# GpSimd's scalings written with a second operation, times one, in a hybrid SSD, attention and FFN layer

## The chip, the cores and the metric

The kernel runs on one core of one Trainium2 chip, as one launch. Its time is device microseconds (us). The median of three runs of the kernel before is 1222.43 us (1222.42 to 1225.11).

## What is computed

One layer of an encoder trunk over 1024 tokens of width 1024, in float32: a modulated RMSNorm, one input projection, a Mamba-2 SSD group of 8 heads beside a chunked attention group of 8 heads, an output projection, a second modulated RMSNorm, a gated feed-forward part with a short causal convolution, and a final RMSNorm. The change lies in two places of it:

```python
def rmsnorm(x, w):
    y = xf * lax.rsqrt(jnp.mean(xf * xf, axis=-1, keepdims=True) + EPS)
...
def chunk_attention(q, k, v, rel_bias):
    scores = jnp.einsum('bcqhd,bckhd->bhcqk', qc, kb) * (ATTN_HEAD_DIM ** -0.5)
    scores = jnp.where(valid, scores + bias[:, None], jnp.finfo(jnp.float32).min)
    p = jax.nn.softmax(scores, axis=-1)
    o = jnp.einsum('bhcqk,bckhd->bcqhd', p, vb)
```

A query sees its own chunk of 64 keys and the 8 chunks before it. The division of the exponentials by their sum, and the addition of EPS to a mean square, are the two operations that the change touches.

## The kernel before

Float32 matrix products are made of three (or two) products of rounded parts: each operand is split into a high and a low part, `mm3` (L75 to L78) issues the three matmuls, and `split` (L80 to L86) makes the parts, as a rule the high part on ScalarE (L85) and the low part on VectorE (L86), in a few calls on GpSimd.

The program has these stages, by the start times of the trace: norm and modulation and the first projections for q, k and v (0 to 103 us); attention over four pairs of heads (103 to 283 us), with the remaining q, k and v projections (`gemm_part`, accumulator `acc`) mixed in; the SSD's convolutions, its projection z and its scan (to about 580 us); the output projection and the feed-forward part (to the end).

Attention for a pair p runs over 8 query tiles of 128 tokens and two heads, 16 probability tiles for each pair and 64 in all. For each tile `attn_scores` does this, with n the number of keys, 128, 256, 384, 512 and then four times 640:

- TensorE: scores into PSUM (`s`, L262), in two buffers;
- VectorE: adds the bias, negates and keeps the row's extreme, from PSUM into the tile `p` in SBUF (L413);
- ScalarE: the exponential in place, and its sum by row (L416);
- VectorE: the reciprocal of that sum, 128x1 (L418);
- GpSimd: the tile times that reciprocal, in place, 128xn (L419).

`attn_pv` then transposes two query tiles of a head on TensorE (`tp`, L445 and L448), splits them on ScalarE and VectorE (`pt`, L85 and L86), multiplies them with the values (`pv`, L456 and L457) and adds two halves into `ya` (L461, L462). `p` has 8 buffers, `s`, `tp` and `tl` have 2, `acc` and `pv` have 1.

GpSimd does besides: two memsets for each of the 8 bias tiles (L475, L476), the low part of six weight tiles in the attention stage (L86, `wl`), and for the norms `rstd` (L113): EPS added to a 128x1 column (L116) and then that column to the power of -0.5 (L117). `rstd` is called for the 8 row tiles of the first norm (L300) and the 8 of the SSD's norm. The second and the final norm use `rstd2`, which adds on VectorE and isn't touched.

The order on each engine's queue isn't that of the source alone: the kernel is built with `schedule_with_timeline_sim=True`, where a planner puts the instructions of all engines in order by costs that it has for each of them, under the dependencies. An engine works its queue strictly in that order.

Of the kernel before, what the change touches and what calls it, by code (L numbers as in the profile page):

```python
# [13 lines left out]
ALU = mybir.AluOpType  # L14
# [50 lines left out]
def tile_block(ctx: ExitStack, tc: tile.TileContext, x, crep, pk, w_ada, w_first, w_ft, w_z,  # L65
# [3 lines left out]
    G = nc.gpsimd  # L69
# [36 lines left out]
    def stat(n=1):  # L106
        if stc[0] + n > 64:
            stc[0] = 0
        a = st1[:, stc[0]:stc[0] + n]
        stc[0] += n  # L110
        return a

    def rstd(ms, eps=EPS):  # L113
        n = ms.shape[-1]
        r = stat(n)
        G.tensor_scalar(ms, ms, eps, None, op0=ALU.add)  # L116
        G.tensor_tensor(r, ms, mhalf[:, 0:n], ALU.pow)  # L117
        return r

# [132 lines left out]
    def scores(p, i):  # L252
        d = qk[p]
        j0 = max(0, i - 4)
        n = (i - j0 + 1) * P
        off = (j0 - (i - 4)) * P
        parts = [(0, n)] if n <= 512 else [(0, 320), (320, 320)]
        st = [s_tile(), s_tile()]
        for h in range(2):
            for pi, (a, w) in enumerate(parts):  # L260
                for ti, kn in enumerate(("kh", "kl")):
                    T.matmul(st[h][:, 512 * pi:512 * pi + w], d["q"][h][:, i * P:(i + 1) * P],  # L262
                             d[kn][h][:, j0 * P + a:j0 * P + a + w], start=ti == 0, stop=ti == 1)
        return st, n, off, parts
# [31 lines left out]
    def norm1(st):  # L296
        ms = stat()
        junk = s0.tile([P, D], F32, tag="junk", name="junk")
        norm_to(xts[st], junk, ms)
        r = rstd(ms)  # L300
        V.tensor_scalar(xts[st], xts[st], r, None, op0=ALU.mult)
# [93 lines left out]
    def p_tile():  # L395
        return pp.tile([P, 640], F32, tag="p", name="p")
# [4 lines left out]
    def attn_scores(p, i, bt):  # L401
        st, n, off, parts = s00 if p + i == 0 else scores(p, i)
        res = []
        for h in range(2):
            pt_ = p_tile()
            nm, rs = stat(), stat()
            if len(parts) == 1:
                src, bsl, dst = st[h][:, 0:n], bt[h][:, off:off + n], pt_[:, 0:n]
            else:
                src = st[h].rearrange("p (a b) -> p a b", a=2)[:, :, 0:320]  # L410
                bsl = bt[h].rearrange("p (a b) -> p a b", a=2)
                dst = pt_.rearrange("p (a b) -> p a b", a=2)
            V.tensor_tensor_reduce(out=dst, in0=src, in1=bsl, scale=-1.0, scalar=3e38,  # L413
                                   op0=ALU.add, op1=ALU.min, accum_out=nm)
            pv_ = pt_[:, 0:n]
            A.activation(pv_, pv_, AF.Exp, scale=-1.0, bias=nm, accum_out=rs)  # L416
            rr = stat()
            last_v[:] = [V.reciprocal(rr, rs).ins]  # L418
            G.tensor_scalar(pv_, pv_, rr, None, op0=ALU.mult)  # L419
            res.append(pt_)  # L420
        return res

# [46 lines left out]
    def attention(p, extra=()):  # L469
        extra = dict(extra)  # L470
        bt = []
        for h in range(2):
            t = bp.tile([P, 640], F32, tag="bias", name="bias")
            nc.sync.dma_start(t, bias[2 * p + h])
            G.memset(t[0:64, 576:640], -1e30)  # L475
            G.memset(t[64:128, 0:64], -1e30)  # L476
            bt.append(t)
        for u in range(4):
            pa = attn_scores(p, 2 * u, bt)
            pb = attn_scores(p, 2 * u + 1, bt)  # L480
            for fn in extra.get(u, ()):
                fn()
            if p == 3:
                if u < 2:
                    early[4 + 2 * u] = wu_pair(w_ft[4 + 2 * u], A, G)
                for _ in range(MODS[u]):
                    mod_col(todo.pop(0), mtq[len(todo) % 4], last_v[0])
            for h in range(2):
                attn_pv(p, u, h, pa[h], pb[h])
# [345 lines left out]
    def ssd_norm(c, y, t, at=None):  # L835
        with tc.issue_after(at) if at else ExitStack():
            V.tensor_tensor(y, y, zs[:, c, 0:512], ALU.mult)
        ms = stat()
        A.activation(t, y, AF.Square, accum_out=ms)
        r = rstd(ms, 512.0 * EPS)  # L840
        A.activation(y, y, AF.Copy, scale=r)
# [708 lines left out]
```

## Time and profile before

| | |
|---|---|
| median of 3 runs | 1222.43 us |
| profiled execution: span on the core | 1221.2 us |
| instructions | 15631 |
| TensorE matmul (PE) busy | 1167.3 us, 96% |
| VectorE (DVE) busy | 928.8 us, 76% |
| ScalarE (ACT) busy | 592.0 us, 48% |
| GpSimd (POOL) busy | 174.3 us, 14% |
| L419, 64 instructions | 99.0 us |
| L116, 16 instructions | 6.4 us |

The result gives no time of the profiled execution beside its span; the span is 1.2 us below the median of the timed runs. Shares are averages over stages that differ: most of GpSimd's 174.3 us lie between 103 and 283 us. In the rows of the views, a line number stands for a line of the kernel, `out<-in` are the tiles by name, and the engine named behind an arrow is the one whose work ended the wait.

### The profile page before, as it was taken

How to read it: one execution, taken by the hardware profiler on the slowest of the kernel's cores; microseconds unless marked ns; L12 is line 12 of the kernel's file. 1: busy time of each engine (PE TensorE's matmuls, PEld its weight loads, DVE VectorE, ACT ScalarE, POOL GpSimd, SP SyncE). 2: the span in 40 equal slices, each digit the busy share in tenths (PEclk: the TensorE clock that was granted, in tenths of full speed). 3: DMA queues.
4: the chain of work that ended last, by engine and by line, in shares of the span. 5: the costliest groups of instructions: out<-in, count | busy, mean ns of one | idle time of the engine just before them, and what ended most of it. 6: DMA issues, size and time to landing. Idle time of an engine off the chain costs nothing.

```text
span 1221.2 us, 15631 instructions
## 1 busy us (share of the span) xinstructions
PE 1167.3 (96%) x5802; PEld 974.5 (80%) x5802; DVE 928.8 (76%) x1402; ACT 592.0 (48%) x993; POOL 174.3 (14%) x166
## 2 busy tenths in 40 slices
PE   5998899989999989999999999999999999999995
PEld 3877787878889978888788888888888888888884
DVE  7846454686697678657999988898889769666976
ACT  4636454664243766676544543344343445433443
POOL 1205463672000125200000000000000000000001
PEclk9999999999999999999999999999999999999998
DMA  9722211311476200141223223322233278633533
GB/s 331 259 56 63 66 54 46 111 58 51 164 246 229 88 18 35 61 147 52 70 104 118 93 107 113 129 79 86 95 129 112 108 250 305 242 126 116 171 114 137
DMA packets 56395, 150.86 MB, mean 124 GB/s; under 512 B 5632, under 2 KB 5760, under 8 KB 54912
## 3 DMA queue, kind: packets, MB, share of 16 engines
q1 hardware_dynamic: 49264, 125.49, 30.4%
q10 hardware_dynamic: 7056, 24.38, 5.0%
q8 instruction: 45, 0.74, 0.2%
q14 instruction: 30, 0.25, 0.1%
HBM read 116.56 MB, written 29.10 MB: 119 GB/s over the span
## 4 chain that ended last, share of the span: by engine, by line
PE 82%; DVE 9%; ACT 3%; issue 2%; DMA 2%; POOL 1%; SPq 0%; DVEq 0%; POOLq 0%; ACTq 0%
PE dn L76 6%; PE dn L77 6%; PE dn L78 6%; PE wops L699 5%; PE uY L76 4%; PE uY L78 4%; PE uY L77 4%; PE uX L78 3%; PE uX L76 3%; PE uZ L77 3%; PE uZ L76 3%; PE uX L77 3%; PE uZ L78 3%; PE s L76 3%; PE s L77 3%; PE s L78 3%
## 5 line engine op out<-in xcount | busy, mean ns | idle before, releaser
L77 PE MATMUL dn<-w 128*128 128x512 f32 x308 | 112.6, 391 | 0.0
L76 PE MATMUL dn<-w 128*128 128x512 f32 x308 | 112.6, 391 | 0.0
L931 POOL TENSOR_TENSOR st<-st,mhalf 128x1 f32<-128x1 f32 x16 | 10.9, 683 | 696.1 <-DVE st L930 684.6
L419 POOL TENSOR_SCALAR p<-p,st 128x640 f32<-128x640 f32 (+4 forms) x64 | 99.0, 1560 | 43.7 <-DVE st L418 36.4
L78 PE MATMUL dn<-w 128*128 128x512 f32 x308 | 103.7, 390 | 0.0
L76 PE MATMUL uY<-tH,w 128*128 128x512 f32 x248 | 97.2, 392 | 0.0
L77 PE MATMUL uY<-tL,w 128*128 128x512 f32 x248 | 97.0, 391 | 0.0
L78 PE MATMUL uY<-tH,w 128*128 128x512 f32 x248 | 96.9, 391 | 0.0
L85 ACT ACTIVATE w<-ya 128x1024 fp32r<-128x1024 f32 (+1 forms) x41 | 39.2, 956 | 87.4 <-PE uY L78 84.2
L699 PE MATMUL wops<-hH,yhl 128*128 128x512 f32 x224 | 74.1, 399 | 2.9 <-DVE yhl L86 1.5
L76 PEld LDWEIGHTS dn<-w 128*128 128x128 f32 x308 | 57.8, 188 | 12.9
L78 PEld LDWEIGHTS dn<-w 128*128 128x128 f32 x308 | 57.8, 188 | 12.8
L77 PEld LDWEIGHTS dn<-w 128*128 128x128 f32 x308 | 57.8, 188 | 12.7
L85 ACT ACTIVATE w<-xs 128x1024 fp32r<-128x1024 f32 (+1 forms) x41 | 39.1, 953 | 37.3 <-PE uY L78 33.3
L78 PEld LDWEIGHTS uY<-tH,w 128*128 128x128 f32 x248 | 46.5, 188 | 10.5
L76 PEld LDWEIGHTS uY<-tH,w 128*128 128x128 f32 x248 | 46.6, 188 | 10.3
L77 PEld LDWEIGHTS uY<-tL,w 128*128 128x128 f32 x248 | 46.6, 188 | 10.2
L413 DVE CUSTOM_DVE_ANT_0 p<-s,bias 128x640 f32<-128x640 f32 (+4 forms) x64 | 40.4, 651 | 17.5 <-PE tp L445 5.2
L76 PE MATMUL s<-hH,wh 128*128 128x512 f32 x128 | 50.1, 392 | 2.2 <-ACT xst L518 2.0
L86 DVE TENSOR_TENSOR pt<-tp,pt 128x512 fp32r<-128x512 f32 (+2 forms) x72 | 41.5, 595 | 13.1 <-ACT pt L85 12.8
L699 PEld LDWEIGHTS wops<-hH,yhl 128*128 128x128 f32 x224 | 41.8, 188 | 12.2 <-DVE yhl L86 1.9
L1101 DVE SCALAR_TENSOR_TENSOR a<-cv,pkt,a 128x1023 f32<-128x1023 f32 (+1 forms) x40 | 51.0, 1278 | 0.1
(453 smaller groups left out, 3388.9 us busy)
## 6 DMA issues: line engine op xcount, KB each, us to landing
wos<-in_w_ada_dram SPq DMA_DIRECT2D x25, 512.0 KB, 4.5
gz<-a ACTq DMA_DIRECT2D x10, 1024.0 KB, 5.0
ya<-in_w_up_dram SPq DMA_DIRECT2D x11, 768.0 KB, 4.1
xs<-in_w_up_dram SPq DMA_DIRECT2D x11, 768.0 KB, 4.2
adat<-in_w_ada_dram SPq DMA_DIRECT2D x16, 512.0 KB, 5.9
raws<-in_w_ft_dram SPq DMA_DIRECT2D x14, 512.0 KB, 4.0
gy<-a ACTq DMA_DIRECT2D x10, 512.0 KB, 2.6
qk<-in_x_dram SPq DMA_DIRECT2D x8, 512.0 KB, 6.6
```

Of the source, the lines that this page charges most:

```text
L76: T.matmul(ps, lh, rh, start=start, stop=False, skip_group_check=more)
L77: T.matmul(ps, lh, rl, start=False, stop=False, skip_group_check=more)
L78: T.matmul(ps, ll, rh, start=False, stop=stop, skip_group_check=more)
L85: i = A.activation(hi, src, AF.Copy) if ehi is A else ehi.tensor_copy(hi, src)
L86: return i, elo.tensor_tensor(lo, src, f32(hi), ALU.subtract)
L413: V.tensor_tensor_reduce(out=dst, in0=src, in1=bsl, scale=-1.0, scalar=3e38, op0=ALU.add, op1=ALU.min, accum_out=nm)
L419: G.tensor_scalar(pv_, pv_, rr, None, op0=ALU.mult)
L699: i = op(*a, **k)
L931: G.tensor_tensor(r, ms, mhalf[:, 0:1], ALU.pow)
L1101: V.scalar_tensor_tensor(a[:, j:S], c[:, 0:S - j], w[2 - j], a[:, j:S], op0=ALU.mult, op1=ALU.add)
```

## The change

Two GpSimd instructions get a second operation, a multiplication by the constant 1.0, in the same instruction. Their number, their operands in memory and what they compute stay.

```diff
@@ rstd @@
-        G.tensor_scalar(ms, ms, eps, None, op0=ALU.add)
+        G.tensor_scalar(ms, ms, eps, 1.0, op0=ALU.add, op1=ALU.mult)
         G.tensor_tensor(r, ms, mhalf[:, 0:n], ALU.pow)
...
@@ attn_scores @@
             last_v[:] = [V.reciprocal(rr, rs).ins]
-            G.tensor_scalar(pv_, pv_, rr, None, op0=ALU.mult)
+            G.tensor_scalar(pv_, pv_, rr, 1.0, op0=ALU.mult, op1=ALU.mult)
```

The planner has another order for the changed program. On TensorE it is the same up to the first attention pair and again from the SSD scan's first tiles on; between these, rows are moved on all engines, and none is added or left out.

TensorE, the first attention pair, behind the scores of its first query tiles: L262 makes scores, L445 and L448 transpose `p` for the two query tiles of a pass, L456 and L457 multiply with the values. Before:

```order
L262 MATMUL s<-qk 128x320 x2
L445 MATMUL tp<-ident,p 128x128
L262 MATMUL s<-qk 128x320 x6
L445 MATMUL tp<-ident,p 128x128
L262 MATMUL s<-qk 128x320 x4
L456 MATMUL pv<-pt,v 128x256
L457 MATMUL pv<-pt,v 128x256
L456 MATMUL pv<-pt,v 128x128
L457 MATMUL pv<-pt,v 128x128
L262 MATMUL s<-qk 128x320 x4
L448 MATMUL tp<-ident,p 128x128
L445 MATMUL tp<-ident,p 128x128
```

The same place after the change:

```order
L445 MATMUL tp<-ident,p 128x128
L262 MATMUL s<-qk 128x320 x4
L445 MATMUL tp<-ident,p 128x128
L448 MATMUL tp<-ident,p 128x128
L445 MATMUL tp<-ident,p 128x128
L448 MATMUL tp<-ident,p 128x128 x3
L262 MATMUL s<-qk 128x320 x4
L456 MATMUL pv<-pt,v 128x256
L457 MATMUL pv<-pt,v 128x256
L456 MATMUL pv<-pt,v 128x128
L457 MATMUL pv<-pt,v 128x128
L262 MATMUL s<-qk 128x320 x8
```

The transposes of the fourth query tile (L448), which stood behind two more score tiles and a product with the values, now stand directly behind the L445 of the same pass. Further on, the first transposes of the third pass (tile `p_1085` by the numbered names) now stand ahead of the second half of the `acc` product of the first `gemm_part`, where they stood behind it.

GpSimd, the end of the first pair and the start of the second, as one piece of the difference, with the buffers' numbers (`p_1195` and `p_1200` are the last tiles of the first pair, `p_1289` to `p_1310` the first of the second; `wl_1323` is the low part of a weight tile, `bias_1856` a bias tile):

```order
 L419 TENSOR_SCALAR p_1195<-p_1195,st1_72 128x640
+L476 MEMSET bias_1856 64x64
 L419 TENSOR_SCALAR p_1200<-p_1200,st1_72 128x640
-L475 MEMSET bias_1856 64x64
-L476 MEMSET bias_1856 64x64
+L419 TENSOR_SCALAR p_1289<-p_1289,st1_72 128x128
 L86 TENSOR_TENSOR wl_1323<-raws_68,wh_1605 128x1024
-L419 TENSOR_SCALAR p_1289<-p_1289,st1_72 128x128
 L419 TENSOR_SCALAR p_1294<-p_1294,st1_72 128x128
 L419 TENSOR_SCALAR p_1305<-p_1305,st1_72 128x256
 L419 TENSOR_SCALAR p_1310<-p_1310,st1_72 128x256
-L86 TENSOR_TENSOR wl_1323<-raws_68,wh_1903 128x1024
```

The memsets of a bias tile come ahead of the last scalings, the first scaling of the second pair passes the weight split, and the next weight split falls behind two more scalings.

## The prediction

> **What bounds the kernel now.** I read the page first, from its sums to the chain, to see which engine sets the end.
>
> ```profile
> PE 1167.3 (96%) x5802; PEld 974.5 (80%) x5802; DVE 928.8 (76%) x1402; ACT 592.0 (48%) x993; POOL 174.3 (14%) x166
> POOL 1205463672000125200000000000000000000001
> PE 82%; DVE 9%; ACT 3%; issue 2%; DMA 2%; POOL 1%; SPq 0%; DVEq 0%; POOLq 0%; ACTq 0%
> ```
>
> TensorE is busy for 96% of the span and makes 82% of the chain that ended last; GpSimd makes 1% of it. So the kernel is bound by TensorE, and a change on GpSimd can only be worth what TensorE now loses by waiting for it, or would lose. The row of tenths says where that can be: GpSimd works between the fourth and the tenth slice, the attention stage. The table of stages cuts that part out.
>
> ```profile
> 103.00:120.00 17.00, 13.49 (x82) 10.78 (x80) 13.45 (x47) 14.15 (x37) 15.19 (x16) 1.00 0.00 1
> 120.00:137.00 17.00, 15.40 (x85) 13.22 (x86) 7.40 (x22) 7.40 (x16) 11.79 (x11) 1.00 0.12 40
> 137.00:185.00 48.00, 45.78 (x276) 39.33 (x274) 26.60 (x73) 27.86 (x65) 26.84 (x20) 1.00 0.24 66
> 185.00:245.00 60.00, 55.88 (x320) 47.94 (x320) 32.99 (x89) 33.44 (x76) 31.38 (x22) 0.97 0.25 83
> 245.00:270.00 25.00, 21.40 (x149) 18.07 (x148) 22.04 (x65) 19.63 (x49) 18.02 (x15) 1.00 0.14 52
> 270.00:283.00 13.00, 13.00 (x68) 11.03 (x67) 9.69 (x20) 3.55 (x8) 11.80 (x5) 1.00 0.14 48
> ```
>
> Behind the window and its length stand the busy times of PE, PEld, DVE, ACT and POOL, then the granted clock. TensorE is idle for 17.00 - 13.49 = 3.51 us in the first row, then 1.60, 2.22, 4.12, 3.60 and 0: 15.05 us in all. That is the ceiling of any gain in attention, 1.2% of the time. In the first row GpSimd is the busiest engine of the core (15.19 of 17 us); in the next four it has 28% to 48% to spare, and in the last TensorE is full anyway.
>
> Next, the waits. First what TensorE's idle time is put down to in 103 to 120 us, then the three largest in 137 to 245 us, then the largest in 245 to 270 us.
>
> ```profile
> PE s L262 <- DVE st L413: 2.7, 7, 0.7
> PE tp L445 <- POOL p L419: 0.7, 1, 0.7
> ```
>
> ```profile
> PE acc L76 <- DVE qk L239: 2.2, 4, 0.8
> PE acc L76 <- DVE qk L232: 1.3, 2, 0.8
> PE s L262 <- DVE st L413: 1.0, 3, 0.4
> ```
>
> ```profile
> PE tp L448 <- DVE pt L86: 1.2, 2, 0.7
> ```
>
> TensorE names GpSimd once, for 0.7 us; the rest is VectorE, which frees score buffers, accumulators and transposes. GpSimd is behind that only in so far as late tiles put VectorE's later work off. GpSimd's own queue shows how near it is to the bound in the first pair:
>
> ```profile
> 103.84 0.63 POOL L419 TENSOR_SCALAR p<-p,st 128x128 f32<-128x128 f32 x1 [0.34 <-DVE st L418]
> 105.99 0.93 POOL L419 TENSOR_SCALAR p<-p,st 128x256 f32<-128x256 f32 x1 [0.47 <-DVE st L418]
> 107.51 17.65 POOL L419 TENSOR_SCALAR p<-p,st 128x256 f32<-128x256 f32 x11 [0.59 <-DVE st L418]
> 125.54 3.75 POOL L419 TENSOR_SCALAR p<-p,st 128x640 f32<-128x640 f32 x2
> ```
>
> From 107.51 us on eleven scalings run without a gap, two memsets, and two more until 129.29 us: GpSimd is the limit of the first pair, and TensorE escapes it because the queue has `acc` products in between.
>
> **The change, part by part: the duration.** No instruction is added, so the first question is what one GpSimd tensor_scalar costs with its second slot filled. The trace has no such instruction. The nearest rows are these:
>
> ```profile
> L419 POOL TENSOR_SCALAR p<-p,st 128x640 f32<-128x640 f32 x32 | 63.9, 2012 | 6.0 <-DVE st L418 5.1 <-PE pv L457 0.8
> L419 POOL TENSOR_SCALAR p<-p,st 128x512 f32<-128x512 f32 x8 | 13.1, 1650 | 11.1 <-DVE st L418 11.1
> L419 POOL TENSOR_SCALAR p<-p,st 128x128 f32<-128x128 f32 x8 | 4.9, 610 | 12.4 <-DVE st L418 7.2 <-PE acc L78 4.9
> L811 POOL TENSOR_TENSOR yy<-xs,pkt 128x512 f32<-128x512 f32 x8 | 10.8, 1359 | 10.1 <-PE s L77 9.9 <-PE xps L699 0.2
> L116 POOL TENSOR_SCALAR st<-st 128x1 f32<-128x1 f32 x16 | 6.4, 401 | 62.4 <-ACT junk L268 39.9 <-ACT yt L839 22.3
> masks.py:199 POOL TENSOR_SCALAR_AFFINE_SELECT ident<-ident 128x128 f32<-128x128 f32 x1 | 0.3, 294 | 0.0
> masks.py:197 POOL MEMSET ident<- 128x128 f32 x1 | 0.2, 205 | 0.3 <-POOLq L1538 0.3
> L123 POOL MEMSET mhalf<- 128x8 f32 x1 | 0.1, 105 | 0.0
> ```
>
> Two undisturbed 640s take 3.75 us, 1.87 us each; against the 610 ns of 128 columns that is (1870 - 610) / 512 = 2.46 ns for a column, over a fixed part near 0.3 us. A memset pays (205 - 105) / 120 = 0.83 ns for a column, the select, which reads, tests and writes, about (294 - 105) / 128 = 1.48 ns. And 128x512 with two inputs is shorter on average (1359 ns) than a scaling of one input (1650 ns). So the single-operation form is dear out of line with what it reads and writes: its 2.46 ns are spent in how that form is worked, and not in ports. Another form may then be worked by another loop, and the bounds lie on both sides. Below: 0.83 ns, the cheapest pass in the trace. Above: a second pass like the first, 4.92 ns. I take the select's 1.48 ns, the nearest row in kind (one input read, something computed, written). A step up of one memset pass, to 3.29 ns, is the rival below.
>
> At 1.48 ns the 64 scalings have 32 x 640 + 8 x (128 + 256 + 384 + 512) = 30,720 columns, and lose 30,720 x 0.98 ns = 30 us of GpSimd's time, 7.5 us for each pair. A 640 would take about 1.25 us.
>
> **What of that reaches the end.** First pair, 103 to 120 us: GpSimd steps down from 15.19 us by about 4,480 columns x 0.98 ns = 4.4 us to 10.8, and ScalarE is late next, with 14.15 of 17 us; that leaves 17.00 - 14.15 = 2.85 us. I take 2, since TensorE's queue also carries latencies that no engine's sum shows. 120 to 137 us: nothing, since its one long wait is for an accumulator:
>
> ```profile
> 129.57 0.47 PE L76 MATMUL acc<-hH,wh 128*128 128x512 f32 x1 [1.51 <-DVE qk L232]
> ```
>
> 137 to 245 us: 6.34 us idle, of which the two accumulator rows above are 3.5, and GpSimd doesn't touch them. The rest hangs on when VectorE comes to its splits; tiles that are ready 0.6 us earlier move that a little: I take 1. 245 to 270 us: VectorE is the busiest (22.04 of 25, so at most 2.96 us to be had), and GpSimd shortens only the way of a tile: 1. The last row: 0, TensorE is full.
>
> The sixteen additions of epsilon are 128x1, all fixed cost (L116, 401 ns on average). They stand in a chain to the norms, and a tenth of a microsecond more or less in each, by the difference between memsets of 8 and 128 columns, is at most 1.6 us either way; I take 0, since half of them are in the SSD stage, where no TensorE wait names them, and leave the 1.6 us to the range.
>
> The moved rows are the other half. The planner's new order puts transposes forward, which is only good if the tiles are there. At the old speed they nearly are: 11 scalings from 107.51 us put `p_995` at about 107.51 + 0.93 + 2 x 1.25 + 1.56 = 112.5 us, where the transposes now stand, and `p_1085` at 112.5 + 1.6 + 3 x 1.87 = 119.7 us, while the second half of the `acc` product, now behind that tile's transposes, began at 120.09 us:
>
> ```profile
> 120.09 0.50 PE L76 MATMUL acc<-hH,wh 128*128 128x512 f32 x1 [0.15 <-DVE qk L232]
> ```
>
> So the order alone costs about nothing there, 0 to 1 us, with 0.4 us of slack. Between 283 us and the SSD scan it also moves rows, with no row that says to which side; I take 0 and keep 3 us on both sides.
>
> Sum: 2 + 1 + 1 = 4 us. Span 1221.2 - 4 = 1217.2, and with the 1.2 us by which the median lies above the span, **1218.4 us**.
>
> **Rivals.** (1) The second operation costs a pass of its own. Price by the memset's slope, 0.83 ns a column. Place: the transposes of `p_1085`, ahead of the `acc` product. Before it stand 2 x (128 + 256 + 384 + 512) + 3 x 640 = 4,480 columns of scaling, 3.7 us more, against 0.4 us of slack: TensorE stands 3.3 us. It decides from 0.4 us / 4,480 = 0.09 ns a column on. The last pair, with 29.8 us of GpSimd work in the 38 us from 245 to 283, loses about 3 more in latency: 1222.4 + 6 = 1228.7 us. At the upper bound, 2.46 ns more, it is 10.6 us at the first place, and 18.9 us more work in the 8.2 us left of the last, so about 10.7 there: 1244 us. For it: GpSimd's time is in its loop. Against it: the loop is slower than any port needs, which a fuller form may not share.
>
> (2) The instruction takes as long as before, and only the order changes: 1222.4, or up to 4 us more, 1226.4, where transposes wait and the later rows move the wrong way. The Trainium skill has a rule for this (GPSIMD Engine Reference, section Performance versus the Vector engine, Elementwise — side-by-side cycle accounting): loop bodies of one or two operations on an element are bound by the ports, at 1.03 cycles for an element, so that a second one is free. At the 1.2 GHz that the page gives, that is an estimate of 0.86 ns a column. The trace doesn't agree with its rate, 2.46 ns against 0.86, so I trust its conclusion little; by it this rival would be the forecast.
>
> (3) The instruction is faster, and it is hidden: TensorE's named waits are for VectorE, and stay. 1220 to 1222 us. The waits above speak for it, the gapless first pair against it.
>
> (4) Faster, but the moved rows lose more than attention gains: 3 us in the convolutions and 3 more in the scan's first tiles, against 1 or 2: 1226.4 to 1227.4.
>
> **How the numbers follow.** The forecast has a chance of 0.50, over times from 1210 (two thirds of the 15.05 us idle) to 1218.7. Rival 3 has 0.14; rival 2 0.10, of it 0.06 within 0.3%; rival 1 0.21; rival 4 0.05. A measurement of this kernel can tell about 0.3%, 3.7 us, from no change, so the bounds are 1218.7 and 1226.1. Faster 0.50; same 0.14 + 0.06 = 0.20; slower 0.21 + 0.04 + 0.05 = 0.30. The range must take in rivals 2 to 4 and the lower half of rival 1: 1210 to 1232. What is left out, the upper half of rival 1 and the ends of the forecast's own spread, is under 0.2. The forecast's own range is 1210 to 1218.7.
>
> **What would show it.** Right, if a 128x640 of L419 is near 1.25 us and L419's 99.0 us near 69; if GpSimd has gaps in the first pair that end at L418; if 103 to 120 us holds more TensorE work than 13.49 us. The duration is wrong if L419 rises, and then TensorE waits for `p` by name at L445 ahead of `acc`. The way to the end is wrong if L419 falls and TensorE's idle time up to 270 us stays near 15 us. The order is to blame if the stages from 283 us on get longer than before.

## The result, and the profile after

The changed kernel's median is 1221.12 us (1218.42 to 1225.33, 22 runs), that of the kernel before beside it 1224.34 us (1221.96 to 1229.63, 22 runs). The ratio is 0.9973, with a 95% interval of 0.9966 to 0.9981: 0.0027 x 1224.34 = 3.3 us less. A second measurement (below) gave 0.9964 (0.9946 to 0.9982). The forecast was 4 us less. All runs here read some 2 us above the three of the table ahead, so the forecast's absolute 1218.4 us was missed by 2.7 us and its difference by 0.7.

The page of the changed kernel, its first line and GpSimd's row of tenths:

```profile
PE 1170.2 (96%) x5802; PEld 977.4 (80%) x5802; DVE 929.8 (76%) x1402; ACT 592.9 (49%) x993; POOL 123.7 (10%) x166
...
POOL 1202232440000135200000000000000000000001
```

GpSimd falls by 50.6 us, from 174.3 to 123.7, and its fourth to ninth slices from 5, 4, 6, 3, 6, 7 tenths to 2, 2, 3, 2, 4, 4. No other engine's sum moves by more than 3 us. The groups say where it went, first L419 as a whole, then by shape:

```profile
L419 POOL TENSOR_SCALAR p<-p,st 128x640 f32<-128x640 f32 (+4 forms) x64 | 45.9, 723 | 76.4 <-DVE st L418 66.2 <-PE tp L448 7.7 <-PE pv L456 1.5
```

```profile
L419 POOL TENSOR_SCALAR p<-p,st 128x640 f32<-128x640 f32 x32 | 28.2, 887 | 21.7 <-DVE st L418 19.4 <-PE pv L456 1.5 <-PE s L262 0.6
...
L116 POOL TENSOR_SCALAR st<-st 128x1 f32<-128x1 f32 x16 | 6.9, 431 | 61.1 <-ACT junk L268 40.0 <-ACT yt L839 20.9
L419 POOL TENSOR_SCALAR p<-p,st 128x512 f32<-128x512 f32 x8 | 6.4, 796 | 17.0 <-DVE st L418 15.4 <-PE tp L448 1.5
...
L419 POOL TENSOR_SCALAR p<-p,st 128x128 f32<-128x128 f32 x8 | 3.0, 372 | 10.5 <-DVE st L418 10.4
```

L419 takes 45.9 us where it took 99.0, and 66.2 of the 76.4 us of GpSimd's idle time ahead of it now end at L418, VectorE's reciprocal: GpSimd waits for tiles. Its queue in the first pair shows the same; in square brackets stands the idle time ahead of the row and what ended it.

```profile
107.97 1.04 POOL L419 TENSOR_SCALAR p<-p,st 128x256 f32<-128x256 f32 x2 [0.79 <-DVE st L418]
...
112.31 0.69 POOL L419 TENSOR_SCALAR p<-p,st 128x512 f32<-128x512 f32 x1 [2.43 <-DVE st L418]
...
117.49 0.81 POOL L419 TENSOR_SCALAR p<-p,st 128x640 f32<-128x640 f32 x1 [1.07 <-DVE st L418]
...
125.51 0.80 POOL L419 TENSOR_SCALAR p<-p,st 128x640 f32<-128x640 f32 x1
```

An undisturbed 640 takes 0.80 us, against 1.87. The pair's last scaling ends at 126.3 us, against 129.29. The stages, in the columns of the prediction's table, come from the second profiled run of the changed kernel (span 1219.0 us), because the first (1222.4 us) was, as shown below, one of the slower executions:

```profile
103.00:120.00 17.00, 14.17 (x89) 11.61 (x89) 15.51 (x54) 15.20 (x39) 8.48 (x15) 1.00 0.08 23
120.00:137.00 17.00, 15.86 (x81) 13.28 (x81) 6.79 (x19) 7.16 (x17) 5.99 (x10) 0.90 0.13 48
137.00:185.00 48.00, 45.78 (x272) 39.65 (x270) 26.57 (x71) 28.48 (x63) 15.20 (x20) 1.00 0.20 58
185.00:245.00 60.00, 56.42 (x328) 48.81 (x329) 33.12 (x93) 33.45 (x78) 18.33 (x22) 0.97 0.27 85
245.00:270.00 25.00, 22.03 (x146) 18.61 (x147) 22.41 (x66) 19.02 (x47) 10.36 (x14) 1.00 0.12 43
270.00:283.00 13.00, 13.00 (x70) 11.00 (x69) 9.89 (x17) 4.54 (x8) 5.23 (x5) 1.00 0.13 40
```

TensorE's idle time is now 2.83, 1.14, 2.22, 3.58, 2.97 and 0: 12.74 us in all, where it was 15.05. (Two of the rows, with clocks of 0.90 and 0.97, hold a stretch at half clock, in which busy time is longer for the same work; before only the fourth did.) What it waits for from 100 to 285 us, first before, then in this run of the changed kernel (us in all, times, longest):

```profile
PE s L262 <- DVE st L413: 4.7, 11, 1.1
...
PE tp L445 <- POOL p L419: 0.7, 1, 0.7
```

```profile
PE tp L445 <- POOL p L419: 1.8, 2, 1.0
PE s L262 <- DVE st L413: 1.3, 5, 0.4
```

The large wait that went is the one for score buffers, which VectorE's bias pass L413 frees: 4.7 to 1.3 us. The waits for GpSimd's own tiles did not fall; they rose from 0.7 to 1.8. Behind attention, before and then after:

```profile
283.00:411.00 128.00, 126.00 (x737) 110.23 (x736) 92.44 (x145) 49.76 (x84) 0.94 (x3) 1.00 0.53 177
```

```profile
283.00:411.00 128.00, 127.27 (x749) 111.52 (x748) 92.93 (x147) 51.48 (x92) 1.54 (x2) 1.00 0.52 177
```

Another 1.27 us of idle time is gone there (0.46 in the first profiled run, with 126.46 us busy). At the first matmul into the tile `uX`, behind the scan, the kernel before stands at 569.4 us and this run at 567.1:

```profile
L58 PE MATMUL uX<-b11h,w x16: 392/394/394, 569.4 to 574.7; 128*128 128x512 f32 x16
```

```profile
L58 PE MATMUL uX<-b11h,w x16: 393/394/394, 567.1 to 572.5; 128*128 128x512 f32 x16
```

These 2.3 us are the whole difference of the spans (1221.2 - 1219.0 = 2.2). From there to the end both take 651.8 to 651.9 us.

Fixed windows mix the gain with the moment at which a stretch begins, and with its stretches at half clock. A measure by work is cleaner: the time from TensorE's 481st matmul, just ahead of the first one that moved (the 489th), to its last product with the values (L457, at 320.4 us before), with time at half clock counted half. It is 214.2 us before, 211.0 in this run of the changed kernel and 210.7 in the first: 3.2 to 3.5 us less. From there to the first matmul into `uX` it is 247.2 us before, 247.2 in this run and 246.2 in the first. So by work the gain lies in attention, and the idle time that is gone between 283 and 411 us is no sure gain of its own. The 2.2 us between the spans are then made of 0.7 us by which this run happens to reach the 481st matmul sooner (103.8 us against 104.5; the first run is there at 105.1), plus 3.2, less 1.7 for one half-clock window more.

**Why two executions of one program differ by 3.4 us.** These are windows of 4 us on TensorE (window, length, busy time, matmuls, granted clock), first of the changed kernel's first profiled run, then of its second:

```profile
107.00:111.00 4.00, 3.69 (x14) 0.58 0.00 0
```

```profile
107.00:111.00 4.00, 4.00 (x29) 1.00 0.01 2
...
119.00:123.00 4.00, 3.25 (x9) 0.66 0.42 141
```

From 107 to 111 us the one has 14 matmuls at a mean clock of 0.58, the other 29 at 1.00, and has its own low stretch at 119 us. The 534th matmul, a transpose of the second pass, starts so, in the same order of runs (1.2 of the 2.55 us are the later start of attention; the rest goes with the low window):

```profile
116.12 0.31 PE L445 MATMUL tp<-ident,p 128*128 128x128 f32 x1
```

```profile
113.57 0.31 PE L445 MATMUL tp<-ident,p 128*128 128x128 f32 x1
```

The record of the clock has it as windows of 3.41 us, sometimes two in a row, in which the clock is 0.5. One costs up to 3.41 / 2 = 1.7 us. Before the last 15 us of the program the kernel before has two such windows in its profile, the second run of the changed kernel three, and the first run four stretches, one of them double. What comes ahead of such a window are gaps, of which none needs to be long. These are the 3.41 us just ahead of one, in the changed kernel's first run, then in the kernel before, and with it a stretch of the kernel before that no low window follows:

```profile
104.25:107.66 3.41, 1.92 (x9) 1.00 0.00 0
```

```profile
237.98:241.40 3.42, 2.29 (x15) 1.00 0.93 329
...
115.41:118.83 3.42, 2.37 (x16) 1.00 0.00 0
```

TensorE is idle for 1.49 and 1.13 us in the first two, in pieces, and for 1.05 us in the third. But the length of the idle time does not decide it alone: in the kernel before TensorE is idle for 1.71 of the 3.41 us from 333.6 to 337.0 us, in one piece, and the clock stays at 1.00 behind it. Among the timed runs of the kernel before in the second measurement, span and mean granted clock go together (correlation -0.93 over 20 runs). So below, beside each ratio, the mean of span times granted clock of the timed runs is given where it matters ("the span net of the clock"): a microsecond at half clock counts half in it, and since the clock is on record to 0.001, one run's figure is good to some 0.6 us. It is 1212.84 us before and 1209.06 us for the changed kernel in the same comparison.

### The profile page after: what moved, and what is told of

Read it like the earlier page. It is cut to its first block, busy times and chain, and to the rows that moved or that the text cites. A ratio compares the mean times of both kernels' runs of the same rounds, so it can differ in the third digit from the quotient of the medians.

```text
span 1222.4 us, 15637 instructions
## 1 busy us (share of the span) xinstructions
PE 1170.2 (96%) x5802; PEld 977.4 (80%) x5802; DVE 929.8 (76%) x1402; ACT 592.9 (49%) x993; POOL 123.7 (10%) x166
## 4 chain that ended last, share of the span: by engine, by line
PE 71%; DVE 5%; ACT 1%; DMA 1%; issue 0%; POOL 0%; DVEq 0%; POOLq 0%; ACTq 0%; SPq 0%
PE wops L699 6%; PE dn L76 6%; PE dn L77 6%; PE dn L78 6%; PE uY L76 4%; PE uY L78 4%; PE uY L77 4%; PE uX L78 3%; PE uX L76 3%; PE uZ L77 3%; PE uZ L76 3%; PE uX L77 3%; PE uZ L78 3%; PE s L76 3%; PE s L77 3%; PE s L78 3%
## 5 line engine op out<-in xcount | busy, mean ns | idle before, releaser
L413 DVE CUSTOM_DVE_ANT_0 p<-s,bias 128x640 f32<-128x640 f32 (+4 forms) x64 | 40.7, 652 | 25.3 <-PE tp L445 9.0
L419 POOL TENSOR_SCALAR p<-p,st 128x640 f32<-128x640 f32 (+4 forms) x64 | 45.9, 723 | 76.4 <-DVE st L418 66.2
```

The costliest lines, as they stand in the source:

```text
L419: G.tensor_scalar(pv_, pv_, rr, 1.0, op0=ALU.mult, op1=ALU.mult)
```

## The experiments

**1. The instruction alone.** At the end of the kernel before, 64 GpSimd instructions are added, four of each of 16 forms, on tiles of their own:

```diff
+        for o in d:
+            pin(G.tensor_scalar(o, a, r, None, op0=ALU.mult))
+        for o in d:
+            pin(G.tensor_scalar(o, a, r, 1.0, op0=ALU.mult, op1=ALU.mult))
+        for o in d:
+            pin(G.tensor_scalar(o, a, r, 0.0, op0=ALU.mult, op1=ALU.add))
+        for o in d:
+            pin(G.tensor_scalar(o, a, r, -8.0, op0=ALU.mult, op1=ALU.max))
...
```

> The kernel before with 64 more GpSimd instructions behind its end, on tiles of their own, each form four times at the end of the queue; the output is untouched and the run is some 70 us longer. What is wanted is the time of one. Theory A1 (any second operation takes the fast loop): at 128x640, one operation 1.87 us, with a column or with a constant; all pairs (times 1.0, plus 0.0, maximum) 0.80 us. Theory A2 (only a multiplication by a constant one is fast): plus 0.0 and maximum at 1.87 us or more. Theory A3 (a column as the scalar is the slow part): one operation with a constant at 0.80 us. The copy, one input and no arithmetic, near 0.6 us; a multiplication of two tiles 1.3 to 1.5 us.

The rows, `pa` the input, `pr` a column that scales it; the lines are in the order of the list that follows:

```profile
L1515 POOL TENSOR_SCALAR pd<-pa,pr 128x640 f32<-128x640 f32 x4 | 9.7, 2420 | 0.4
L1509 POOL TENSOR_SCALAR pd<-pa,pr 128x640 f32<-128x640 f32 x4 | 7.5, 1892 | 0.0
L1521 POOL TENSOR_SCALAR pd<-pa 128x640 f32<-128x640 f32 x4 | 7.2, 1815 | 0.0
...
L1511 POOL TENSOR_SCALAR pd<-pa,pr 128x640 f32<-128x640 f32 x4 | 3.1, 799 | 0.0
L1513 POOL TENSOR_SCALAR pd<-pa,pr 128x640 f32<-128x640 f32 x4 | 3.1, 798 | 0.0
...
L1523 POOL TENSOR_SCALAR pd<-pa 128x640 f32<-128x640 f32 x4 | 2.8, 723 | 0.0
L1529 POOL COPY pd<-pa 128x640 f32<-128x640 f32 x4 | 2.7, 718 | 0.0
L1533 POOL TENSOR_SCALAR pd<-pa,pr 128x128 f32<-128x128 f32 x4 | 2.3, 601 | 0.0
L1535 POOL TENSOR_SCALAR pd<-pa,pr 128x128 f32<-128x128 f32 x4 | 1.4, 372 | 0.0
L1537 POOL TENSOR_SCALAR pd<-pa 128x1 f32<-128x1 f32 x4 | 0.8, 218 | 0.0
L1539 POOL TENSOR_SCALAR pd<-pa 128x1 f32<-128x1 f32 x4 | 0.6, 190 | 0.0
```

In this order: times a column, then the maximum with -8 (2420 ns); times a column alone (1892); plus a constant alone (1815); times a column, times 1.0 (799); times a column, plus 0.0 (798); plus a constant, times 1.0 (723); a copy (718). Then 128x128 alone and with times 1.0 (601, 372), and 128x1 with an addition, alone and with times 1.0 (218, 190). A pair of multiplications or additions runs at (799 - 372) / 512 = 0.83 ns for a column, and a 640 of it takes about as long as a copy (723 to 799 against 718 ns); the single operation and the pair with a maximum take 2.4 and 3.0 times as long. None of the three theories holds as it stands: the second operation need not be a multiplication by one, but not every second operation helps. What is read and written is the same in all three, so the difference lies in how GpSimd works the form; that it is another loop is a guess that no run shows.

**2. The new form in the old order.** The changed kernel, each engine's queue held in the order of the kernel before by dependencies that carry no wait:

```diff
+ORDER = "..."
...
+def keep_order(tc):
...
+                tc.add_manual_dep(i, prev.name, mybir.DependencyInfo(
+                    mybir.DependencyClass.NoSync, mybir.DependencyReason.DATA), reason="order")
```

> The two-operation form on both lines, with every engine's queue held in the order of the kernel before. Theory A (the shorter instruction carries the gain): L419 at 128x640 stays near 0.80 us and 1.5 to 3.5 us come off, ratio 0.9971 to 0.9988. Theory B (the moved rows carry it, and a shorter instruction in the old order only makes GpSimd idle longer): 0.9992 to 1.0005, with GpSimd's gaps grown and TensorE's idle time between 103 and 270 us still near 15 us.

In the traces the kernels held like this, here and in experiments 3 and 6, have the same sequence of operations and tiles on TensorE, VectorE, ScalarE and GpSimd as the kernel whose order they hold, and as many instructions in all (15631 and 15637). So the holding itself adds no work that could explain a difference.

Measured: 0.9982 (0.9969 to 0.9995); the span net of the clock is 1212.14 us against 1212.94. By the ratio that is within theory A, and its interval overlaps that of the changed kernel. Net of the clock it is 0.8 us, where the changed kernel has 3.8 (experiment 5). Attention itself is no shorter: by the measure by work it takes 214.3 us, against 214.2 before, so where the 0.8 us lie is not shown. TensorE waits for score buffers as before:

```profile
PE s L262 <- DVE st L413: 4.8, 11, 1.4
```

**3. The old form in the new order.** The kernel before, held in the order of the changed kernel in the same way.

> The one-operation form on both lines, with every engine's queue in the order of the changed kernel. Theory A: the transposes that were put forward wait for tiles that come at 1.87 us each; the waits of L445 and L448 for L419 grow from 0.7 us to 2 to 6 us, ratio 1.001 to 1.005. Theory B: the moved rows alone give the gain, ratio near 0.997. The prediction's working has 0 to 1 us for the order at its first place, ratio 1.000 to 1.001.

Measured: 1.0019 (1.0004 to 1.0035), net of the clock 1212.80 against 1212.94 us. Its last two stages, and TensorE's waits from 100 to 285 us:

```profile
245.00:270.00 25.00, 21.87 (x137) 18.53 (x136) 19.29 (x58) 17.60 (x43) 15.70 (x14) 0.93 0.11 40
270.00:283.00 13.00, 11.21 (x57) 9.54 (x56) 10.99 (x24) 4.69 (x13) 13.00 (x6) 0.87 0.24 81
```

```profile
PE s L262 <- DVE st L413: 2.0, 5, 0.8
PE tp L448 <- POOL p L419: 1.9, 3, 1.0
```

The order takes the waits for score buffers from 4.7 to 2.0 us with the old form too. But TensorE now waits for GpSimd's tiles in their place: 1.9 us at L448, where it had no such wait, 1.2 of them in the first pair and 0.7 in the last; with 0.7 at L445, as before, that is within theory A. In the last stage GpSimd is busy for all of 13.00 us, and TensorE idle for 1.79 of a stretch that it filled before. By the measure by work attention takes 214.1 us, against 214.2 before: what one wait gives, the others take. All waits of TensorE that the view names from 100 to 285 us sum up to 14.7 us before, 14.2 in experiment 2, 14.9 here and 12.0 in the changed kernel. Each of these two stages also has a half-clock window, at 1.7 us (0.07 x 25 and 0.13 x 13).

**4. Epsilon alone, and the scalings alone.** In the first only L116 has the second operation, and the order is that of before; in the second only L419 has it, and the order is that of the changed kernel.

```diff
-            G.tensor_scalar(pv_, pv_, rr, 1.0, op0=ALU.mult, op1=ALU.mult)
+            G.tensor_scalar(pv_, pv_, rr, None, op0=ALU.mult)
```

> Only the addition of epsilon has the second operation; the order on all engines is that of the kernel before. Theory A and theory B both: ratio 0.9992 to 1.0008, since 16 instructions of 128x1 change by a tenth of a microsecond at most. A ratio under 0.9985 would mean that the norms' chain, not attention, gives part of the gain.

Measured: 0.9990 (0.9978 to 1.0002), net of the clock 1212.68 against 1212.94 us: no difference that can be told. Attention takes 214.2 us by work, as before.

```diff
-        G.tensor_scalar(ms, ms, eps, 1.0, op0=ALU.add, op1=ALU.mult)
+        G.tensor_scalar(ms, ms, eps, None, op0=ALU.add)
```

> The scaling L419 in the two-operation form, the addition of epsilon in the old form; the order of each engine is that of the changed kernel. Theory, the scalings alone make the gain: ratio 0.9960 to 0.9985, like the changed kernel's. Rival, the additions of epsilon carry part of it: ratio between 0.9985 and 1, and the changed kernel's gain is not reached.

Measured: 0.9968 (0.9956 to 0.9981), with 211.0 us for attention by work, as in the changed kernel. The scalings are the change.

**5. The changed kernel once more,** to have a second profile of it and a second ratio.

> The changed kernel itself, beside the kernel before and the variants below on one chip, to part the clock from the work: for each run, span times mean granted clock. Theory A with the order as its partner (the shorter instruction gives little in the old order, the new order gives nothing with the long one, both together give the gain): ratio 0.996 to 0.998, and span times clock 3 to 4 us below that of the kernel before. If the gain seen so far was one of the clock's, span times clock differs by less than 1 us.

Measured: 0.9964 (0.9946 to 0.9982), net of the clock 1209.06 against 1212.84 us, and the profile that is shown above.

**6. A slower form in the new order.** Here the second operation of L419 is a maximum with -8, the slowest row of experiment 1, which leaves the values as they are (they lie above it); the order is held as in the changed kernel.

```diff
-            G.tensor_scalar(pv_, pv_, rr, 1.0, op0=ALU.mult, op1=ALU.mult)
+            G.tensor_scalar(pv_, pv_, rr, -8.0, op0=ALU.mult, op1=ALU.max)
```

> The changed kernel, its order held on every engine, with the maximum with -8 as the second operation of L419 in place of the multiplication by one (the probabilities are positive, so the values stay). By the run of the forms it takes 2.42 us for 128x640 where the old form takes 1.87, about 0.85 ns more for a column: the price that the prediction's first rival had. Theory R (that rival's sum is right): 6 us above the kernel before, ratio 1.005, with TensorE waiting some 3 us for L419 ahead of the acc product of the first pair. Theory S (GpSimd's gaps take most of it up): ratio 1.002 or less. By the run with the old form in the new order, 1.0019, I expect R or more.

Measured: 1.0098 (1.0079 to 1.0118) over four runs, 12.9 us more, twice what was expected. It is rival 1, built: by experiment 1 the second operation adds (2420 - 1892) / 640 = 0.83 ns a column. Its groups, its waits from 100 to 285 us, TensorE's queue at the place that the rival named, and the last two stages:

```profile
L419 POOL TENSOR_SCALAR p<-p,st 128x640 f32<-128x640 f32 x32 | 80.2, 2506 | 3.9 <-DVE st L418 1.3
```

```profile
PE tp L448 <- POOL p L419: 6.0, 4, 2.7
PE s L262 <- DVE st L413: 5.2, 5, 4.2
```

```profile
123.41 0.40 PE L448 MATMUL tp<-ident,p 128*128 128x128 f32 x1 [2.69 <-POOL p L419]
...
125.32 0.63 PE L77 MATMUL acc<-hL,wh 128*128 128x512 f32 x1
```

```profile
245.00:270.00 25.00, 18.52 (x120) 15.79 (x119) 15.71 (x47) 14.54 (x38) 17.59 (x13) 0.93 0.15 61
270.00:283.00 13.00, 9.98 (x60) 8.15 (x59) 10.77 (x32) 8.08 (x19) 12.55 (x6) 1.00 0.26 82
```

TensorE stands 2.69 us at the transposes of the third pass with the accumulator product behind them, as rival 1 had it (3.3 us), and the product then starts at half clock (0.63 us for a matmul that takes 0.39). In the last two stages it is idle for 9.50 us where it was for 3.60. Net of the clock the kernel loses 3.3 us (1216.12 against 1212.84); the timed runs lose 18.2 us to the clock, before loses 9.5. So by these means 8.7 of 12.0 us of the loss are half-clock windows that come with the stalls. In the profiled runs alone it is less: 1218.4 against 1212.6 us net of the clock, 5.9 of the 13.5 us between the spans, so more than half of the loss is the clock's by either count.

**7. Using the freed GpSimd.** First, the 64 reciprocals of L418 on GpSimd, as a power of -1, so that GpSimd no longer waits for VectorE; then, in another kernel, the low parts of the two weight tiles that the kernel leaves to VectorE (at p == 2). Both are the changed kernel otherwise, in the order that the planner gives them.

```diff
+    mone = const.tile([P, 8], F32, name="mone")
+    G.memset(mone, -1.0)
...
-            last_v[:] = [V.reciprocal(rr, rs).ins]
+            G.tensor_tensor(rr, rs, mone[:, 0:1], ALU.pow)
```

> The changed kernel with the 64 reciprocals moved from VectorE to GpSimd, as a power of -1 on a 128x1 column (0.55 us each by the rows of L117 and L931), so that a tile goes from ScalarE to GpSimd without VectorE between; the planner has its own order for it. GpSimd would have 46 + 35 = 81 us of work in 180, VectorE 9 us less. Theory A (what is left is VectorE's lateness: L413, L418 and the evacuations of acc): ratio to the kernel before 0.994 to 0.996. Rival: the way of a tile grows by 0.4 us on GpSimd and nothing is won: 0.997 to 1.000.

Measured: 1.0031 (1.0020 to 1.0041), slower, where 0.994 to 0.996 and, by the rival, 0.997 to 1.000 was expected.

```diff
-        if p == 2 and which < 2:
+        if False:
```

> The changed kernel with the low parts of two more weight tiles on GpSimd (2.39 us each) in place of VectorE (1.23 us each), in the time that the shorter scalings leave free. Theory A: VectorE is the next bound at the start of attention, ratio to the kernel before 0.996 to 0.997. Rival: these tiles are made before attention, where VectorE isn't waited for: 0.997, the changed kernel's own.

Measured: 0.9981 (0.9967 to 0.9995), not told apart from the changed kernel, whose interval overlaps it. Neither beats it.

**8. Why the reciprocals lost.** The loss of the first lies in the feed-forward part, which has no reciprocal of L418: in 650 to 1200 us, where TensorE is never idle, it has 2383 matmuls, the kernel before 2399. What is left to differ are addresses: the constant column of 8 floats moves all later tiles by 32 bytes. Three kernels test that. The first widens the new column to 16 floats, so that the tiles lie 64 bytes further; the others are the changed kernel with `mhalf` widened to 16 and to 24 floats, with no instruction and no order changed.

```diff
-    mone = const.tile([P, 8], F32, name="mone")
+    mone = const.tile([P, 16], F32, name="mone")[:, 0:8]
```

```diff
-    mhalf = const.tile([P, 8], F32, name="mhalf")
+    mhalf = const.tile([P, 16], F32, name="mhalf")[:, 0:8]
```

> The reciprocals on GpSimd once more, with the constant column that they use widened from 8 to 16 floats, so that every tile that is allocated behind it lies 32 bytes further; each engine's order is that of the run recip_gpsimd. Theory A, the matmuls of the feed-forward part were slowed from 390 to 392 ns because the 32 bytes of the constant shifted the addresses of the later tiles: its stage from 573 us to the end is again about 648.3 us and the ratio about 0.9995 (0.9975 to 1.001). Theory B, the slower feed-forward part comes from the moved reciprocals or their order: the ratio stays near 1.003 and the stage near 652 us.

> The changed kernel with the constant mhalf widened from 8 to 16 floats: the tiles allocated behind it lie 32 bytes further, and no instruction or order differs. Theory A (addresses off 64 bytes slow the matmuls): the stage from 573 us to the end is some 652 us in place of 648.3, and the ratio about 0.9997 (0.998 to 1.002). Theory B (addresses don't matter): the ratio of the changed kernel, 0.9964 to 0.9973, and 648.3 us.

> The changed kernel with the constant mhalf widened from 8 to 24 floats: the tiles allocated behind it lie 64 bytes further, no instruction or order differs. In 650 to 850 us, where TensorE is never idle, the changed kernel has 873 matmuls, the 32 byte shift 868, the run with reciprocals and a 64 byte shift 871. Theory A (only an offset off 64 bytes costs): 873 or 874 matmuls, and the changed kernel's ratio, 0.9964 to 0.9973. Theory B (a part of the cost has a longer period, 128 bytes or more): 871, and a ratio near 0.9985 (0.997 to 1.000). Theory C (any shift costs alike): 868 and 1.0003.

Measured: 1.0000 (0.9986 to 1.0014) for the reciprocals moved on, 1.0003 (0.9991 to 1.0015) for the changed kernel shifted by 32 bytes, and 0.9976 (0.9962 to 0.9991) for a shift by 64. TensorE from 650 to 1200 us (matmuls in brackets, then the clock), in the changed kernel, with 32 bytes and with 64:

```profile
650.00:1200.00 550.00, 550.00 (x2399) 1.00 0.40 140
```

```profile
650.00:1200.00 550.00, 550.00 (x2384) 1.00 0.39 138
```

```profile
650.00:1200.00 550.00, 550.00 (x2393) 1.00 0.39 139
```

At full clock and without a gap the same matmuls go through 15 of 2399, 0.63%, slower, or 4.1 us over the 650 us from 572 us on; at 64 bytes it is 6, or 1.6 us. The run with the shift by 64 was on another chip than the others of these experiments, but the reciprocals with 64 bytes, on the same chip as the rest, have 2393 too. So a shift of 32 bytes costs as much as the change brings, and one of 64 bytes isn't free either. The kernel before, the changed one and those of experiments 2 to 5 have 2399 each, that of experiment 6 has 2398, so none of their differences comes from there. With tiles moved by 64 bytes in both, the reciprocals on GpSimd (1.0000) are not better than the changed kernel (0.9976); that they are worse is likely, but the intervals meet.

## Why the prediction was right, and where it was not

**The bound and the ceiling** held: all that was won is idle time of TensorE, 2.3 us of the 15.05 up to 283 us and 0.5 to 1.3 more up to 411 us; by work it is 3.2 to 3.5 us in attention. (One slip: the forecast's lower end, 1210 us, was called two thirds of the idle time. It is 12.4 us below 1222.4, or 82% of it; two thirds would be 1212.4.)

**The duration** was right in direction and mis-sized. Taken were the select's 1.48 ns a column, 1.25 us for a 640 and 69 us for L419; it is 0.83 ns, 0.80 us and 45.9 us, the lower bound of the range. That one operation is dear for how it is worked, and not for what it reads and writes, is shown by experiment 1: the pair reads and writes the same and takes 799 ns against 1892. The Trainium skill's rule that was set against the forecast (GPSIMD Engine Reference, Performance versus the Vector engine, Elementwise — side-by-side cycle accounting), an estimate of 0.86 ns a column for one or two operations, fits the pair; it doesn't fit one operation, at (1892 - 601) / 512 = 2.52 ns, so what was concluded from it, that the second is free and the time stays, missed a gain of 53 us of GpSimd's time.

**What reaches the end** was put too large for what GpSimd loses: 4 us out of 30, where 3.2 to 3.5 us came out of 53. The forecast's 2 + 0 + 1 + 1 us stand against 0.7 + 0.5 + 0.5 + 0.6 = 2.3 us of idle time in the table up to 283 us (the first of these holds the 0.7 us by which that run began attention sooner). In the first stage I let ScalarE, at 14.15 of 17 us, come late next with 2.85 us to win. But the work that moved into the stage brought VectorE from 13.45 to 15.51 us and ScalarE to 15.20, so that the room was half of that. For 283 us onward I put 0 with 3 us either way. By work nothing, or 1.1 us in the first run, is won behind the last product with the values, so 0 was about right.

**How it reaches the end** is the step that failed, and that the total came within 1 us is luck in part: a loss of GpSimd's time that was put too small, times a share of it that was put too large, by a way that experiment 2 doesn't show. The sum gave the gain to tiles that are ready sooner, and to the order 0 to 1 us of cost. The two orders and two forms, as ratios to before:

| | old order | new order |
|---|---|---|
| one operation | 1 | 1.0019 (1.0004 to 1.0035) |
| two operations | 0.9982 (0.9969 to 0.9995) | 0.9964 (0.9946 to 0.9982), 0.9973 (0.9966 to 0.9981) |

Net of the clock they are, against before, 0 (one operation, old order), -0.1 (one, new), -0.8 (two, old) and -3.8 us (two, new); attention by work takes 214.2, 214.1, 214.3 and 211.0 us. Neither part does it alone. The new order takes away 2.7 of the 4.7 us of waiting for score buffers even in the old form (how VectorE's queue does that was not traced); the short instruction is what makes the order affordable, since with the old form TensorE waits for GpSimd's tiles instead. That the order by itself costs 0 to 1 us net was near enough; that the gain comes only with it was not seen, because I looked only at the places where it puts transposes ahead of tiles, and not at the wait for score buffers that headed the list.

**Epsilon**: 0 taken, 0.9990 (0.9978 to 1.0002) measured, and 28 ns for each of 16 by experiment 1, 0.4 us if all stood on the path. In the kernel the mean of L116 did not even fall (401 ns before, 431 after).

**The rivals.** (1) Its mechanism and place are real when the form is slow (experiment 6), its condition didn't come true, and its price was too low: 6 us worked out, 12.9 measured. What it had not counted are the half-clock windows; net of the clock the loss is 3.3 us by the means of the timed runs and 5.9 in the profiled one. (2) is out by the groups. (3) is right about the old order, where attention is no shorter with the faster instruction. (4) is out, the later rows lost nothing.

**The signs.** L419 at 69 us: 45.9. Gaps on GpSimd that end at L418: they came. More TensorE work than 13.49 us in 103 to 120 us: 14.17 at full clock, but in a run that began attention 0.7 us sooner, so the sign says little; the first run's larger figure there holds a half-clock window, in which the same matmuls are longer, so it can't be read at all. Stages from 283 us on longer than before: none. That the ratio lies at the edge of the 0.3% that a measurement can tell is why the interval (0.9966 to 0.9981) reaches to both sides of it.

## What to carry to other kernels

A wait that is charged to one engine can be shortened by another engine's faster instruction, but here it was so only with the queues ordered anew around it: test form and order apart, and don't expect the gain to be the sum of the two. On GpSimd, time the form that is written, not the operation: here the instruction with a useless second operation was the cheaper one. Before a difference of 0.3% is believed, count the matmuls in a stretch where TensorE is never idle, and look at the granted clock: here a constant of 32 bytes or two half-clock windows weigh as much.

## What was not expected of the hardware

- GpSimd's tensor_scalar is fast for pairs of multiplications and additions (0.83 ns a column, 128x640 in 0.72 to 0.80 us), and slow for a single operation (1.81 to 1.89 us) and for a pair with a maximum (2.42 us).
- TensorE's clock falls to 0.5 for 3.41 us after a stretch that is far from idle: 1.49 and 1.13 us of idle time in 3.41, in pieces, went ahead of two such windows, 1.05 us of another stretch had none, and neither had 1.71 us in one piece, so what sets it off stays open. One program has such windows at 107 us in one execution and at 120 us in the next. A window costs up to 1.7 us.
- The matmuls of the feed-forward part take 0.63% longer when all later tiles lie 32 bytes further, and 0.25% at 64 bytes, with no instruction or order changed. Why, and which tile it is, was not tried.
